# A list-scheduled two-layer encoder: input chunks loaded in natural order, and other priorities in the scheduler

## The chip, the core and the metric

One NeuronCore of a Trainium2 chip runs the whole program. PE (TensorE), DVE (VectorE), ACT (ScalarE) and POOL (GpSimd) each take their instructions in a fixed order; SP (SyncE) issues all DMAs, also in a fixed order. Time is device time of one execution in microseconds (us).

## What is computed

Two sequences of 1024 and 512 tokens get 16 meta tokens each and pass two layers of a hybrid encoder of width 1024. Each layer, cut to its core:

```python
h = rmsnorm(x, pre_g)
aq, ak, av, ag, bq, bk, bv, bg = split(h @ w_in)
oa = window_gqa_attention(rope(aq), rope(ak), av, sink) * silu(ag)   # 8 heads, 2 KV heads, window 128
ob = diff_attention(rope(bq), rope(bk), bv, lam, subln_g) * silu(bg) # 4 heads, softmax - lam * softmax
o = concat(oa, ob) @ w_out
x = x + rmsnorm(o, post_g)
```

All of it is in fp32. The outputs are the tokens without the meta tokens.

## The kernel before

**Tiles.** The 1568 tokens are cut into four chunks of 392. Every fp32 operand of a matmul is split into a high part and the rest, the low part (`hi`, `lo`), and a product is three matmuls: high times high, and high times low both ways. Activations of a chunk stand with their features on partitions (`hT[ci]`, in buffers named `slot`), weights in `whl` (high and low beside each other), two more of the first unit's weights in `kk` and `vv`.

**Stages.** A layer has six units: four heads of differential attention (`attn_b`), then two groups of window attention (`attn_a`). Before a unit comes its input projection (`inproj`, results in `ps_d`, now and then `ps_o`), four to six blocks of weights; its results go through rope or a gate to DRAM and come back as keys `kk`, values `vv` and queries `qq`. Scores stand in `ps_s`, transposes in `ps_t`, attention's products in `ps_o`; `pp` holds probabilities, `at` their transposes, `og` a unit's outputs, which go to `MX` in DRAM. Projections of the next unit fill PE while a unit's softmax runs. Then `outproj` runs steps that a string names: `b` is the first half of the output projection, `s` and `S` the second half with the row's statistics (`norm`), `l` loads half of a mix, `f` fetches the residual, `p` is the post norm with the residual and the next layer's row scale, `n` turns the new rows by transposes into layer 1's `hT`. So `n0` makes chunk 0 of layer 1, and it needs rows of output chunks 0 and 1.

**Start.** Chunk 0 of x is loaded with features on partitions. Its statistics come late and are multiplied in behind the projection (`late`). Before the change chunks 1 to 3 are loaded the same way; `prestats` squares them on ACT or POOL, sums the eight feature blocks on DVE, and `rstd_bc` turns the sums by PE transposes, reduces, takes the root on POOL, and turns them back into `rb`, a tile that has every token's scale on all partitions. `prenorm` then multiplies by gain and `rb` (DVE), copies the high part (ACT) and subtracts it (DVE).

**Order.** Nothing runs in the order of the code. `Recorder` notes every operation with what it depends on, and a list scheduler with modelled costs decides the order on each engine when the program is built: each engine takes the ready operation with the smallest `prio`, which is its place in the code less two numbers:

```python
o.prio = o.seq - self.boost - self.base + self.rnd.random() * SPREAD
```

`boost` is set around single operations (`BOOST_W` weights, `BOOST_M` mix loads, `BOOST_P` the first reading of a projection's result, `BOOST_E` the rest of its evacuation, rope above all), `base` for whole steps (`BASE`, `BASE_A` by unit, `BASE_0` and `BASE_S` for the statistics at the start). An operation made with `any`, `any_copy` or `any_tt` may go to either of two engines. Buffers are pools with fixed numbers of tiles. The profile names all instructions by one line, since one helper issues them; the tiles' names tell them apart.

Of the kernel before, what the change touches and what calls it, by code (L numbers as in the profile page):

```python
# [14 lines left out]
F32R = mybir.dt.float32r  # L15
# [18 lines left out]
    [[(0, 392)], [(392, 392)], [(784, 256), (1056, 120)], [(1176, 392)]],  # L34
# [6 lines left out]
BOOST_W = 300  # L41
BOOST_M = 1000
BOOST_E = 300
BOOST_P = 300
# [4 lines left out]
BASE_0 = 60  # L49
# [3 lines left out]
QUICK = 1  # L53
# [4 lines left out]
COMB = ((1, 1, 1, 1), (1, 1, 1, 1))  # L58
PRE_ACT = (0, 0, 0, 0, 0, 0, 0, 0)
# [4 lines left out]
ONLY = 4  # L64
# [63 lines left out]
ANY = dict(PE=0, ACT=0, DVE=0, POOL=0, SP=0)  # L128
# [414 lines left out]
def hymba_kernel(ctx, tc, xT, xr, w_in, w_out, rope, masks, pre_g, post_g, sub_g, sink_b, sink_m, lam_in, yo):  # L543
# [179 lines left out]
    def prestats(xs, tmp, n, only=False):  # L723
        if only:
            for i in range(4):
                r = slice(2 * (i % 2), 2 * (i % 2) + 2)
                x, y = xs[i // 2][:, r, 0:n], tmp[i // 2][:, r, 0:n]
                nc.any((nc.scalar, "activation", (y, x, AF.Square), {}),
                       (nc.gpsimd, "tensor_tensor", (y, x, x), dict(op=ALU.mult)))
                if i:  # L730
                    nc.vector.tensor_tensor(
                        tmp[0][:, 0:2, 0:n], tmp[0][:, 0:2, 0:n], tmp[i // 2][:, r, 0:n], op=ALU.add)
            nc.vector.tensor_tensor(tmp[0][:, 0, 0:n], tmp[0][:, 0, 0:n], tmp[0][:, 1, 0:n], op=ALU.add)
        else:
# [7 lines left out]
    def scaled(out, x, g, rb, n, act):
        for j in range(x.shape[1]):
            if act:
                nc.scalar.activation(out[:, j, 0:n], x[:, j, 0:n], AF.Copy, scale=g[:, j:j + 1])
                nc.any_tt(out[:, j, 0:n], out[:, j, 0:n], rb[:, 0:n], ALU.mult)
            else:
                nc.vector.scalar_tensor_tensor(
                    out[:, j, 0:n], x[:, j, 0:n], g[:, j:j + 1], rb[:, 0:n], op0=ALU.mult, op1=ALU.mult)

    def prenorm(l, ci, xs, rb, n):
        his, los = [], []
        for i in range(2):
            hi, lo = pair(F32R)
            for j in range(4):
                r = slice(j, j + 1)
                h = at_p([128, 1, CN])
                scaled(h, xs[i][:, r], preg[:, l, 4 * i + j:4 * i + j + 1], rb, n, PRE_ACT[2 * ci + i])
                h = h[:, :, 0:n]
                nc.any_copy(hi[:, r, 0:n], h)  # L760
                if l == 0 and ci < QUICK:
                    nc.vector.tensor_tensor(lo[:, r, 0:n], h, f32(hi[:, r, 0:n]), op=ALU.subtract)
                else:
                    nc.any_tt(lo[:, r, 0:n], h, f32(hi[:, r, 0:n]), ALU.subtract)
# [327 lines left out]
    def attn_a(l, g):  # L1092
        S = SC[l]
        AK, AV, AQ = S["AK"][g], S["AV"][g], S["AQ"][g]
        for s in range(2):
# [53 lines left out]
            for c0 in range(0, len(heads), 3):  # L1149
# [26 lines left out]
                nc.extra = [nc.last]  # L1176
# [133 lines left out]
    def outproj(l):  # L1310
# [91 lines left out]
        def stat(parts, M):  # L1402
            r = sm_p([128, 4])
            for u, p in enumerate(parts):
                sq = ru_p([128, 512])
                nc.scalar.activation(sq[0:M], p, AF.Square, scale=1.0 / 32, accum_out=r[0:M, u:u + 1])
            nc.vector.scalar_tensor_tensor(
                r[0:M, 2:3], r[0:M, 0:1], EPS, r[0:M, 1:2], op0=ALU.add, op1=ALU.add)
            nc.gpsimd.tensor_tensor(r[0:M, 3:4], r[0:M, 2:3], mhalf[0:M, 0:1], op=ALU.pow)
            return r[0:M, 3:4]  # L1410

# [186 lines left out]
```

## Time and profile before

| | |
|---|---|
| median of 3 runs | 1935.77 us (1933.12 to 1939.91) |
| profiled execution | 1938.61 us |
| its span | 1936.8 us |
| busy | PE 95%, DVE 78%, ACT 52%, POOL 14% |
| mean granted clock of PE | 0.985 |

The span runs from the first to the last instruction; the execution's time is 1.8 us more. A wait of PE is idle time with the tile and engine that ended it. The granted clock is a share of PE's full speed.

### The profile page before, as it was taken

The numbers are of one execution on the slowest core, as the hardware profiler recorded it, in microseconds if no ns is written. First come the engines' busy times: TensorE is split into PE (matmuls) and PEld (weight loads), VectorE is DVE, ScalarE is ACT, GpSimd is POOL, SyncE is SP. The second block draws the span as 40 slices with busy tenths as digits, with TensorE's granted clock in tenths as the row PEclk, the third lists the DMA queues.
The fourth block names the chain that finished last, engine by engine and source line by source line (L and its number), as shares of the span: only waits on it lengthen the run. The fifth ranks groups of instructions, "written<-read, shape, count | busy, mean of one in ns | idle before, by whom it ended". The sixth has DMA issues, their size and how long they took to land.

```text
span 1936.8 us, 35552 instructions
## 1 busy us (share of the span) xinstructions
PE 1843.4 (95%) x12328; PEld 1771.3 (91%) x12328; DVE 1515.2 (78%) x3363; ACT 1008.1 (52%) x2417; POOL 279.3 (14%) x516
## 2 busy tenths in 40 slices
PE   6999999999999989999789999999999999999998
PEld 5989989999989889999789999999999999889998
DVE  8858788888787787587988397787967859869767
ACT  4335445454444475575765254454545438648632
POOL 3001111211121210000221021121111101101001
PEclk8999999999999999999989999999999999999999
DMA  7253363544543657556354535445353475684464
GB/s 252 56 161 105 110 170 102 148 119 109 153 117 108 154 144 198 118 133 178 120 196 116 152 100 160 120 118 161 98 167 114 124 180 125 159 229 99 109 205 150
DMA packets 299147, 273.02 MB, mean 141 GB/s; under 512 B 101560, under 2 KB 263480, under 8 KB 298840
## 3 DMA queue, kind: packets, MB, share of 16 engines
q1 hardware_dynamic: 298968, 270.75, 50.5%
q8 instruction: 98, 1.61, 0.4%
q14 instruction: 81, 0.66, 0.1%
HBM read 149.19 MB, written 96.01 MB: 127 GB/s over the span
## 4 chain that ended last, share of the span: by engine, by line
PE 70%; DVE 11%; DMA 8%; ACT 4%; issue 4%; SPq 2%; POOL 1%; DVEq 0%; POOLq 0%; ACTq 0%
PE ps_d L451 43%; PE ps_s L451 10%; PE ps_o L451 9%; PE ps_t L451 8%; DVE at L451 2%; DVE pp L451 2%; DVE slot L451 2%; ACT pp L451 2%; SPq L451 2%; DVE sm L451 1%; DMA vv<-BV 1%; DVE og L451 1%; DMA kk<-AK 1%; DVE ru L451 1%; POOL sm L451 1%
## 5 line engine op out<-in xcount | busy, mean ns | idle before, releaser
L451 PE MATMUL ps_d<-slot,whl 128*128 128x392 f32 (+2 forms) x4560 | 938.2, 347 | 15.0 <-ACT slot L451 6.7
L451 PEld LDWEIGHTS ps_d<-slot,whl 128*128 128x128 f32 x4560 | 785.7, 190 | 22.2 <-ACT slot L451 6.7
L451 PE MATMUL ps_s<-kk,qq 128*128 128x264 f32 (+9 forms) x1496 | 284.4, 319 | 21.7 <-ACT pp L451 5.7
L451 PE MATMUL ps_o<-at,vv 128*128 128x256 f32 (+6 forms) x1368 | 285.9, 307 | 8.4 <-DVE og L451 5.5
L451 ACT ACTIVATE at<-ps_t 128x256 fp32r<-128x256 f32 (+9 forms) x434 | 187.7, 439 | 202.7 <-PE ps_t L451 177.4
L451 ACT ACTIVATE pp<-ps_s,sm 116x1040 f32<-116x1040 f32 (+4 forms) x208 | 203.9, 980 | 169.9 <-DVE sm L451 161.5
L451 DVE TENSOR_TENSOR at<-ps_t,at 128x256 fp32r<-128x256 f32 (+6 forms) x472 | 224.5, 480 | 68.0 <-ACT at L451 53.5
L451 PEld LDWEIGHTS ps_s<-kk,qq 128*128 128x128 f32 (+4 forms) x1496 | 227.2, 185 | 46.9 <-ACT pp L451 9.0
L451 PE MATMUL ps_d<-whl,slot 128*128 128x256 f32 x1800 | 259.0, 288 | 8.6 <-DVE slot L451 6.0
L451 PEld LDWEIGHTS ps_d<-whl,slot 128*128 128x128 f32 x1800 | 235.1, 192 | 14.3 <-DVE slot L451 7.2
L451 DVE TENSOR_REDUCE sm<-ps_s 116x1 f32<-116x1040 f32 (+4 forms) x208 | 218.3, 1050 | 34.3 <-PE ps_s L451 33.3
L451 ACT ACTIVATE pp<-pp,sm 128x336 f32<-128x336 f32 (+6 forms) x347 | 206.6, 607 | 61.0 <-DVE sm L451 57.6
L451 PEld LDWEIGHTS ps_o<-at,vv 128*128 128x128 f32 (+1 forms) x1368 | 214.0, 190 | 16.8 <-ACT pp L451 5.4
L451 PE MATMUL ps_t<-ident,pp 128*128 128x128 f32 (+6 forms) x1248 | 203.5, 269 | 3.1 <-DVE at L451 1.6
L451 POOL TENSOR_TENSOR pad<-pp,pad 128x64 fp32r<-128x64 f32 (+3 forms) x145 | 53.2, 370 | 819.0 <-ACT pad L451 528.1
L451 PEld LDWEIGHTS ps_t<-ident,pp 128*128 128x128 f32 (+6 forms) x1248 | 147.8, 137 | 14.7 <-ACT pp L451 2.8
L451 DVE CUSTOM_DVE_ANT_0 pp<-ps_s,mk,nsinks 128x336 f32<-128x336 f32 (+2 forms) x192 | 97.1, 528 | 22.1 <-PE ps_s L451 20.3
L451 POOL TENSOR_TENSOR sm<-sm 128x2 f32<-128x2 f32 (+3 forms) x112 | 48.7, 437 | 408.2 <-DVE sm L451 404.6
L451 POOL TENSOR_TENSOR sm<-sm,mhalf 128x1 f32<-128x1 f32 (+7 forms) x98 | 80.8, 830 | 132.9 <-DVE sm L451 129.6
L451 ACT ACTIVATE og<-ps_o 64x128 f32<-64x128 f32 (+4 forms) x248 | 66.1, 287 | 44.8 <-PE ps_o L451 27.3
L451 ACT ACTIVATE ru<-ps_d 128x392 f32<-128x392 f32 (+5 forms) x100 | 48.7, 487 | 73.9 <-PE ps_d L451 64.2
L451 DVE TENSOR_TENSOR slot<-slot 128x512 f32<-128x512 f32 (+3 forms) x79 | 73.9, 945 | 8.4 <-ACT slot L451 8.0
(158 smaller groups left out, 2130.3 us busy)
## 6 DMA issues: line engine op xcount, KB each, us to landing
wraw<-in_w_in_dram SPq DMA_DIRECT2D x46, 512.0 KB
qq<-qq SPq DMA_DIRECT2D x144, 128.0 KB
BS<-st SPq DMA_DIRECT2D x80, 196.0 KB
qq<-AQ SPq DMA_DIRECT2D x96, 128.0 KB
gl<-GT SPq DMA_DIRECT2D x72, 128.0 KB
MX<-og SPq DMA_DIRECT2D x72, 128.0 KB
slot<-MX SPq DMA_DIRECT2D x11, 768.0 KB
kk<-BS SPq DMA_DIRECT2D x8, 1040.0 KB
```

The source lines that it names most:

```text
L451: fn(*[_real(a) for a in args], **{k: _real(a) for k, a in kw.items()})
```

## The change

It has three parts.

1. Chunks 1 to 3 of x come from `xr`, with tokens on partitions: four tiles of 96 rows (chunks 1 and 2, which become 384 tokens long for layer 0) or 98 rows (chunk 3). `stat` makes each row's scale (two Squares with a running sum on ACT, one small step on DVE, one on POOL), two copies scale the tile, and `turned` turns it with PE: 8 groups of 4 transposes for a chunk. The high part is a copy of the result with the gain, the low part one DVE instruction. `turned` is what step `n` did before, now shared.
2. Numbers of the scheduler: `BOOST_W`, `BOOST_M`, `BOOST_E`, `BOOST_P`, `BASE_0`, `BASE`, `BASE_A`, `COMB` (how many row tiles of a head are combined with an ACT step), a penalty of 200 for DVE where an operation may go to two engines, and the modelled cost of DMAs by their number of rows.
3. In `attn_a` the mask steps no longer depend on the last score matmul of their batch, only on their own.

In all, PE has 96 transposes of chunks more and 24 of statistics fewer; columns of all other matmuls are the same. Instructions on DVE go from 3365 to 3298, on ACT from 1939 to 2012, on POOL from 521 to 535, on SP from 1550 to 1555.

```diff
-    [[(0, 392)], [(392, 392)], [(784, 256), (1056, 120)], [(1176, 392)]],
+    [[(0, 392)], [(392, 384)], [(776, 264), (1056, 120)], [(1176, 392)]],
...
-BOOST_W = 300
-BOOST_M = 1000
-BOOST_E = 300
-BOOST_P = 300
+BOOST_W = 280
+BOOST_M = 1200
+BOOST_E = -700
+BOOST_P = 1300
...
-COMB = ((1, 1, 1, 1), (1, 1, 1, 1))
+COMB = ((1, 1, 1, 3), (1, 1, 1, 1))
-BASE = ({'f': 400, 'p': 100, 's': -100, 'S': 0, 'b': 800}, {'f': 0, 'S': 400})
+BASE = ({'f': 400, 'p': 100, 's': -100, 'S': 0, 'b': 800, 'n': 100}, {'f': 0, 'S': 400})
-BASE_A = ((-200, 1500, 1500, -200, 200, 400), (0, 0, 0, 0, 1500, 0))
+BASE_A = ((-200, 1500, 1500, -200, 200, 400), (-300, 0, 0, 0, 1500, 0))
...
-ANY = dict(PE=0, ACT=0, DVE=0, POOL=0, SP=0)
+ANY = {'PE': 0, 'ACT': 0, 'DVE': 200, 'POOL': 0, 'SP': 0}
...
+                    dma(x[a:b].rearrange("p u d -> p (u d)"), xr[t0:t0 + b - a])
...
+    def stat(parts, M):
+        r = sm_p([128, 4])
+        for u, p in enumerate(parts):
+            sq = ru_p([128, 512])
+            nc.scalar.activation(sq[0:M], p, AF.Square, scale=1.0 / 32, accum_out=r[0:M, u:u + 1])
+        nc.vector.scalar_tensor_tensor(
+            r[0:M, 2:3], r[0:M, 0:1], EPS, r[0:M, 1:2], op0=ALU.add, op1=ALU.add)
+        nc.gpsimd.tensor_tensor(r[0:M, 3:4], r[0:M, 2:3], mhalf[0:M, 0:1], op=ALU.pow)
+        return r[0:M, 3:4]
+
+    def turned(l, tiles, off, n):
...
+                        nc.tensor.transpose(
+                            pt[:, o:o + M], get(u)[:, 128 * k:128 * k + 128], ident[0:M, 0:M])
...
+                nc.any_copy(hi[:, k, 0:n], p, g)
                 nc.vector.scalar_tensor_tensor(
+                    lo[:, k, 0:n], p, g, f32(hi[:, k, 0:n]), op0=ALU.mult, op1=ALU.subtract)
...
-                nc.extra = [nc.last]
                 for bi, (u, i) in enumerate(batch):
...
+            for x in xin[ci]:
+                r = stat([x[0:n // 4, u] for u in range(2)], n // 4)
+                for u in range(2):
+                    nc.any_copy(x[0:n // 4, u], x[0:n // 4, u], r)
```

The order on ACT at the start, from the first weight's high part (the first `whl<-pp`) on; `slot<-slot,preg` are chunk 0's high parts, `slot<-slot` squares of chunks 0 and 1. Before:

```order
L451 ACTIVATE whl<-pp 128x1024
L451 ACTIVATE slot<-slot,preg 128x392 x6
L451 ACTIVATE slot<-slot 128x784 x3
L451 ACTIVATE slot<-slot,preg 128x392 x2
L451 ACTIVATE slot<-slot 128x784 x2
L451 ACTIVATE whl<-pp 128x1024
L451 ACTIVATE kk<-pp 128x1024
L451 ACTIVATE vv<-pp 128x1024
```

After; `ru,sm<-slot` are the new Squares with a sum, on tiles of chunk 1:

```order
L448 ACTIVATE whl<-pp 128x1024
L448 ACTIVATE slot<-slot,preg 128x392 x6
L448 ACTIVATE slot<-slot 128x784 x3
L448 ACTIVATE slot<-slot,preg 128x392 x2
L448 ACTIVATE ru,sm<-slot 96x512 x5
L448 ACTIVATE whl<-pp 128x1024
L448 ACTIVATE slot<-slot,sm 96x512 x3
L448 ACTIVATE ru,sm<-slot 96x512 x2
L448 ACTIVATE kk<-pp 128x1024
```

Between chunk 0's last high part and the second weight's stand five Squares, where two squares of two blocks stood.

The order on PE at the start; `ps_d<-slot,whl`, `ps_o<-slot,kk` and `ps_d<-slot,vv` are products of the projection, `ps_t<-ident,sm` the statistics' way back. Before, from the last products of chunk 0 on:

```order
L451 MATMUL ps_d<-slot,vv 128x392 x18
L451 MATMUL ps_t<-ident,ru 98x128 x4
L451 MATMUL ps_t<-ident,slot 98x128 x4
L451 MATMUL ps_t<-ident,sm 128x98 x4
L451 MATMUL ps_t<-ident,slot 94x128 x4
L451 MATMUL ps_o<-slot,whl 128x392 x3
```

After, from the first instruction on; `ps_t<-ident,slot 128x96` are the new transposes of chunk 1:

```order
L448 MATMUL ps_d<-slot,whl 128x392 x24
L448 MATMUL ps_t<-ident,slot 98x128 x4
L448 MATMUL ps_d<-slot,whl 128x392 x9
L448 MATMUL ps_t<-ident,sm 128x98 x4
L448 MATMUL ps_d<-slot,whl 128x392 x9
L448 MATMUL ps_o<-slot,kk 128x392 x3
L448 MATMUL ps_d<-slot,whl 128x392 x3
L448 MATMUL ps_o<-slot,kk 128x392 x3
L448 MATMUL ps_t<-ident,slot 128x96 x8
```

Chunk 1's first instructions with its features stood behind all 96 products of chunk 0 with the four weights (the 18 above and 78 ahead of them), and stand behind 54 of them now.

The order on PE at the layer boundary, from the last products of attention (`ps_o`) to layer 1's first transposes (`ps_t<-ident,slot`); `ps_d<-whl,slot` and `ps_d<-whl,at` are products of the output projection, 128x256 each. Before:

```order
L451 MATMUL ps_o<-at,kk 128x256
L451 MATMUL ps_d<-whl,slot 128x256 x3
L451 MATMUL ps_o<-at,vv 128x512
L451 MATMUL ps_d<-whl,slot 128x256 x12
L451 MATMUL ps_t<-ident,slot 128x128 x12
L451 MATMUL ps_d<-whl,slot 128x256 x30
L451 MATMUL ps_t<-ident,slot 128x128 x8
```

After:

```order
L448 MATMUL ps_o<-at,vv 128x512
L448 MATMUL ps_d<-whl,slot 128x256 x21
L448 MATMUL ps_d<-whl,at 80x256 x24
L448 MATMUL ps_d<-whl,slot 128x256 x90
L448 MATMUL ps_d<-kk,at 80x256 x3
L448 MATMUL ps_d<-whl,slot 128x256 x3
L448 MATMUL ps_d<-kk,at 80x256 x3
L448 MATMUL ps_d<-whl,slot 128x256 x3
L448 MATMUL ps_d<-kk,at 80x256 x6
L448 MATMUL ps_d<-vv,at 80x256 x6
L448 MATMUL ps_d<-kk,slot 128x256 x3
L448 MATMUL ps_t<-ident,slot 128x128 x8
```

The transposes stood 12 matmuls behind the last product of attention, and stand 162 behind it now. Chunk 3's second mix half is first read in the 30 products that stood behind the first 12 transposes; after the change it is first read 115 products behind attention's last one.

The order on SP at the same place; `MX0<-og` stores attention's last outputs, `slot<-MX0` loads chunk 3's mix from them, `X1<-slot` stores rows of layer 0's result. Before:

```order
L451 DMA MX0_152<-og_11952 128x2x128
L451 DMA X1_137<-slot_10734 128x512
L451 DMA X1_137<-slot_10708 128x512
L451 DMA slot_12020<-MX0_152 128x4x384
L451 DMA pp_12024<-PM_138 80x1024
```

After:

```order
L448 DMA wraw_11968<-in_w_in_dram 128x1024
L448 DMA MX0_152<-og_11901 128x2x128
L448 DMA slot_12005<-MX0_152 128x4x384
L448 DMA X1_137<-slot_10815 128x512
L448 DMA pp_12022<-PM_138 80x1024
```

The two stores of X1 that stood between the store and the load are gone from there.

## Rows read from the trace of the kernel before

**Rows 1.** The page: busy time by engine, and the chain that ended last.
```profile
PE 1843.4 (95%) x12328; PEld 1771.3 (91%) x12328; DVE 1515.2 (78%) x3363; ACT 1008.1 (52%) x2417; POOL 279.3 (14%) x516
...
PE 70%; DVE 11%; DMA 8%; ACT 4%; issue 4%; SPq 2%; POOL 1%; DVEq 0%; POOLq 0%; ACTq 0%
```

**Rows 2.** Busy time by stage (windows: stretch, length, engines, PEclk, DMA).
```profile
0.00:120.50 120.50, 98.02 (x519) 92.99 (x520) 89.93 (x162) 43.79 (x72) 22.62 (x22) 0.94 0.54 170
...
640.00:935.00 295.00, 278.56 (x2013) 265.98 (x2012) 228.91 (x693) 187.28 (x542) 25.82 (x57) 0.98 0.60 152
935.00:985.00 50.00, 31.71 (x209) 27.70 (x208) 45.23 (x91) 33.55 (x82) 15.22 (x17) 0.83 0.55 175
985.00:1040.00 55.00, 53.61 (x404) 52.51 (x403) 47.23 (x91) 33.68 (x76) 10.70 (x14) 1.00 0.42 136
```

**Rows 3.** Timeline of PE at the start: time, length, work, idle time before it.
```profile
17.72 2.06 PE L451 MATMUL ps_d<-slot,whl 128*128 128x392 f32 x10 [1.40 <-DVE whl L451]
...
33.34 0.64 PE L451 MATMUL ps_t<-ident,ru 128*98 128x128 f32 x4 [1.42 <-DVE ru L451]
...
40.28 0.91 PE L451 MATMUL ps_t<-ident,sm 98*128 98x98 f32 x4 [5.76 <-POOL sm L451]
```

**Rows 4.** Windows behind the two longest waits, with the granted clock.
```profile
40.00:50.00 10.00, 8.70 (x29) 7.54 (x30) 8.24 (x16) 5.34 (x10) 1.68 (x2) 0.53 0.29 78
...
970.00:985.00 15.00, 8.92 (x39) 7.78 (x40) 11.64 (x19) 8.95 (x15) 2.01 (x3) 0.51 0.88 274
985.00:990.00 5.00, 5.00 (x46) 5.00 (x45) 3.45 (x6) 1.78 (x4) 0.00 (x0) 1.00 0.17 65
```

**Rows 5.** Timeline of PE at the layer boundary.
```profile
960.82 0.40 PE L451 MATMUL ps_o<-at,vv 80*128 80x512 f32 x1
961.05 1.59 PE L451 MATMUL ps_d<-whl,slot 128*128 128x256 f32 x12
...
970.42 1.59 PE L451 MATMUL ps_t<-ident,slot 128*128 128x128 f32 x6 [7.57 <-ACT slot L451]
975.50 1.09 PE L451 MATMUL ps_t<-ident,slot 128*128 128x128 f32 x4 [3.49 <-DVE slot L451]
977.60 0.79 PE L451 MATMUL ps_d<-whl,slot 128*128 128x256 f32 x2 [1.01 <-ACT slot L451]
979.55 5.82 PE L451 MATMUL ps_d<-whl,slot 128*128 128x256 f32 x28 [1.16 <-DVE slot L451]
```

**Rows 6.** Groups of instructions by form, PE, transposes of 98-row results.
```profile
L451 PE MATMUL ps_t<-ident,ru 128*98 128x128 f32 x140 | 21.2, 274 | 3.5 <-ACT ru L451 2.1 <-DVE ru L451 1.4
```

**Rows 7.** Groups by form, ACT: squares at the start, Squares with sum at the boundary.
```profile
L451 ACT ACTIVATE slot<-slot 128x784 f32<-128x784 f32 x8 | 6.4, 844 | 0.1
...
L451 ACT ACTIVATE ru<-slot 128x512 f32<-128x512 f32 x25 | 15.7, 627 | 6.5 <-DVE slot L451 6.2
...
L451 ACT ACTIVATION_READ_ACCUMULATOR ru<-slot 128x1 f32 x25 | 4.6, 186 | 0.0
```

**Rows 8.** Timeline of ACT and of DVE: chunk 3's second mix half.
```profile
976.06 1.48 ACT L451 ACTIVATE slot<-slot 128x1536 fp32r<-128x1536 f32 x1 [1.28 <-DMA slot<-MX]
...
977.75 1.75 DVE L451 TENSOR_TENSOR slot<-slot 128x1536 fp32r<-128x1536 f32 x1
```

**Rows 9.** Waits of PE, 640 to 935 us: total, times, longest.
```profile
PE ps_s L451 <- DMA kk<-AK: 4.6, 3, 2.5
PE ps_o L451 <- DVE og L451: 4.1, 5, 2.7
PE ps_s L451 <- DVE sm L451: 1.9, 3, 0.9
...
PE ps_t L451 <- DVE at L451: 1.3, 2, 1.0
PE ps_s L451 <- DMA qq<-qq: 1.0, 2, 0.6
```

**Rows 10.** Window 1010 to 1035 us, of instructions on transposes' results alone.
```profile
1010.00:1035.00 25.00, 6.72 (x48) 5.72 (x48) 9.13 (x16) 3.93 (x7) 1.00 0.40 125
```

More of the change, by code (lines that the diff above doesn't have):

```diff
@@ L597, in dma @@
             in_ = in_.bitcast(F32)
+        for v in (out, in_):
+            rows = [x for x in v.shape if x > 1] or [1]
+            nc.weight = max(nc.weight, cost * 16 // max(k for k in range(1, 17) if rows[0] % k == 0))
         nc.sync.dma_start(out=out, in_=in_)
@@ L742, in scaled, with prestats @@
[L742 to L747, printed above, removed]
-                nc.vector.scalar_tensor_tensor(
[L749 to L764, printed above, removed]
+    def prestats(xs, tmp, n):
+        for i in range(4):
+            r = slice(2 * (i % 2), 2 * (i % 2) + 2)
+            x, y = xs[i // 2][:, r, 0:n], tmp[i // 2][:, r, 0:n]
+            nc.any((nc.scalar, "activation", (y, x, AF.Square), {}),
+                   (nc.gpsimd, "tensor_tensor", (y, x, x), dict(op=ALU.mult)))
+            if i:
+                nc.vector.tensor_tensor(
+                    tmp[0][:, 0:2, 0:n], tmp[0][:, 0:2, 0:n], tmp[i // 2][:, r, 0:n], op=ALU.add)
+        nc.vector.tensor_tensor(tmp[0][:, 0, 0:n], tmp[0][:, 0, 0:n], tmp[0][:, 1, 0:n], op=ALU.add)
+        return rstd_bc(tmp[0][:, 0, 0:n], n, 1.0 / D)
@@ new lines, in stat @@
+    def stat(parts, M):
[8 more added lines that the diff above has]
+    def turned(l, tiles, off, n):
+        his, los = [], []
+        for u in range(2):
+            hi, lo = pair(F32R)
+            for k in range(4):
+                pt = ps_t([128, 512])
+                o = 0
+                with nc.macro():
+                    for get, M in tiles:
+                        nc.tensor.transpose(
+                            pt[:, o:o + M], get(u)[:, 128 * k:128 * k + 128], ident[0:M, 0:M])
+                        o += M
+                g = preg[:, l, 4 * u + k:4 * u + k + 1]
+                p = pt[:, off:off + n]
+                nc.any_copy(hi[:, k, 0:n], p, g)
+                nc.vector.scalar_tensor_tensor(
+                    lo[:, k, 0:n], p, g, f32(hi[:, k, 0:n]), op0=ALU.mult, op1=ALU.subtract)
@@ L765, in prenorm @@
             his.append(hi)
             los.append(lo)
-        hT[ci] = (rows(his, 4), rows(los, 4))
+        return rows(his, 4), rows(los, 4)
+    def prenorm(ci):
+        n = sum(m for _, m in ICH[0][ci])
+        m = n // 4
+        hT[ci] = turned(0, [(lambda u, x=x: x[0:m, u], m) for x in xin[ci]], 0, n)
     def load_w(src, pool=None, pri=0):
@@ L1400, in outproj @@
         rs = {}
[L1402 to L1410, printed above, removed]
         def norm(ci, j, M):
```

84 lines of the change are left out of this document (34 added, 50 removed).

## The prediction

> **What bounds the kernel now.** I read the page first, then the stages, then the single waits. PE is busy for 1843.4 us of the span of 1936.8 and holds 70% of the chain that ended last [rows 1]. So the time is PE's work plus PE's idle time, and the other engines matter only where PE waits for them. The stages show where that is [rows 2]: of 93 us of idle time, 22.5 lie in the first 120.5 us (120.5 − 98.02), 16.4 in layer 0's window attention (295 − 278.56), 18.3 in the 50 us in which layer 0's output projection turns into layer 1's input (50 − 31.71). The long stretches between have almost none, so a change of order can win nothing there.
>
> At the start the matmuls of chunk 0 with all four weights run on until 33.34 − 1.42 = 31.9 us; then PE waits 1.42 us for DVE and, a few transposes later, 5.76 us for POOL, which makes the reciprocal root of chunk 1's statistics [rows 3]. After that wait the granted clock is 0.53 between 40 and 50 us, near the lower level of 1.2 GHz [rows 4]. At the layer boundary four waits stand in a row: 7.57, 3.49, 1.01 and 1.16 us, 13.2 together [rows 5]. The first two are for the tiles that layer 1's first transposes read, the last two for the two parts of chunk 3's second mix half. Here too the clock falls, to 0.51 from 970 to 985, and is 1.00 behind it [rows 4].
>
> **The change, part by part.** *Input in natural order: what PE gains in work.* Chunks 1 to 3 are now turned by PE: 3 chunks x 8 column blocks x 4 tiles = 96 transposes more. The transposes of the column statistics, 4 out and 4 back per chunk, go: 24 fewer. The order shows both counts. The nearest row has 21.2 us for 140 transposes, 0.151 us each [rows 6], so +14.5 − 3.6 = +10.9. At 0.13 to 0.18 each it would be +9 to +13. Nothing hides this, since PE is the bound: it must be paid by waits.
>
> *What it takes off PE's waits.* The squares summed across eight blocks, the two transposes and the POOL step between give way to two Squares with a running sum per tile on ACT (0.627 + 0.186 us each [rows 7]), a POOL step and two scaled copies. Eight such Squares are 6.5 us of ACT for a chunk; before, four squares of 0.844 us [rows 7] did it on ACT and POOL, with three sums on DVE. But they need no transposes, so PE no longer waits in the middle of a chain for POOL. The first transposes of chunk 1 stand behind 54 projection matmuls, not 96: the rest of chunk 0's work serves as cover between chunk 1's pieces. The 5.76 and the 1.42 us should go, −7.2, and with them the low clock: 8.70 us of busy PE at 0.53 [rows 4] are 4.1 us of lost work, −4.1.
>
> *What it puts in front of the second weight.* PE waits 1.40 us at 17.72 for the low part of weight 1 [rows 3]. On ACT its high part now stands behind five of the new Squares, where two old ones stood (the excerpt shows it): 5 x 0.813 − 2 x 0.844 = +2.4 us [rows 7]. Behind it are queued weight 2 and the copies of chunk 1. DVE, which makes the low part, has one more sum of two blocks ahead of it, but is no longer slowed by POOL squaring chunk 1. Bounds +1 and +3; I take +2. Chunk 1's last tile could come up to 2 us late; the other chunks' projections can be put in between, so I take 0. The start: +10.9 − 7.2 − 4.1 + 2 = **+1.6**; −3 where the shorter waits go too, +12 where the low clock and a wait of the old size come back.
>
> *Layer boundary.* The stage priorities ('n' 100 ahead, mix loads at 1200, ropes and evacuations at −700) move the work. Before, 12 matmuls stand between the last attention product and layer 1's first transposes, and chunk 3's products come behind these. After, 162 output-projection matmuls stand there, and the first use of chunk 3's mix lies 115 behind that last product. The last attention product ends at 961.2. A matmul of this shape takes 1.59/12 = 0.133 us [rows 5]: 115 of them give 15.2 us and 162 give 21.5. When are the operands there? On the trace of before the last scaled tile is in use at 975.5, 14.3 us after that product, and the low part of chunk 3's mix is made by 977.75 + 1.75 = 979.5, 18.3 us after it [rows 5, 8]. So the transposes are covered (21.5 against 14.3) and chunk 3's mix nearly: 18.3 − 15.2 = 3.1 us of wait left. On SP the load of that mix now stands straight behind the store that it reads, where two X1 stores stood between; that is worth under 1 us and I leave it in the bounds. Of 13.2 us of waits 3.1 stay; the low clock goes with the long gap: 8.92 us at 0.51 [rows 4] are 4.4 lost. Together −10.1 − 4.4 = **−14.5**. Bounds: −17.6 with no wait left, −3 if the posts of chunk 0, now later in DVE's row, come last.
>
> *The rest of the tables, and the mask step.* Rope's second half, two or more DVE instructions per chunk and weight, now yields to attention's evacuations. PE waited 4.1 us for the `og` step and 1.3 us for `at` in layer 0's window attention [rows 9]; about half of that, −3, is what a better order on DVE can give. Free operations leave DVE for ACT by the 200 in the scheduler's table; ACT is under two thirds busy in that stage (187 of 295 us [rows 2]) and takes them. The mask step per head lets DVE begin before the last score matmul of a batch; PE's waits on `sm`, 1.9 us [rows 9], bound its gain, and I count nothing: DVE's own two steps behind it hold `ps_s` as long. `COMB` and `BASE_A` move work between engines that do not bind there. Bounds −8 and +5; I take **−3**.
>
> **Sum.** +1.6 − 14.5 − 3 = −15.9. The profiled execution took 1938.6, so 1922.7. It lay 2.8 above the median of the runs, 1935.8, so against runs the same sum gives 1919.9: I say **1920**.
>
> **A rule that speaks against it.** In this trace 48 transposes stand among projection matmuls from 1010 to 1035, 6.72 us of PE's work, and the granted clock is 1.00 throughout [rows 10]. The Trainium skill, "TensorE: Matmul & The Clock Gate", Part 4, says that a transpose does not count as PE activity in the way a matmul does and does not bring the clock up. By that rule the 96 transposes at the start, which stand in groups of 4 and 8 between 3 to 18 matmuls, might hold the clock low there; the row above speaks against it for such a mixture.
>
> **Rivals.**
> *A, the forecast:* 1913 to 1927.
> *B, more is won:* chunk 3's mix comes in time, the short waits before it (5.1 us of the 18.3 at the boundary) go too, and DVE's new order empties `og` and `at` in both layers. −17.6 − 5 − 8 + 1.6 − 2 (the first qq and ACT waits at the end of the start) = −31: about 1905. For it speaks that all of these are waits for DVE or ACT with PE work at hand; against it that DVE is 88% busy in the boundary's two stages (92.5 of 105 us [rows 2]).
> *C, DVE becomes the bound at the boundary:* in its two stages DVE works 45.23 + 47.23 = 92.5 us of 105 [rows 2]. Even without an idle moment the 105 could shrink only by 12.5, unless work leaves the stage; if DVE keeps half of its idle time, the gain is 6, the rest comes back as waits of chunks 1 to 3 of layer 1, and the sum is +1.6 − 6 − 1 = −5.4: 1930, and up to 1936 if the start costs more. The change moves some DVE work to ACT and some rope work out of it, so I hold A above it.
> *D, slower: rope comes too late.* With 1000 less in priority the ropes' ends, their stores and the loads of the next unit's keys and queries behind them on SP come later. PE already waits 4.6 us for `kk` and 1.0 for `qq` in one stage [rows 9], 2.5 at the longest. There are eleven unit starts behind the first; if each waits another 2.5 us it is +27 − 15.9: 1947. It decides from 1.5 us per start, where the whole gain is gone. Against it: the order leaves about the same number of matmuls between a unit's last projection and its first score as before.
> *E, the clock stays low at the start with the transposes:* chunk 1 to 3's transposes lie within some 50 us. If a third to a half of them ran at 0.53, 8 to 12 us would be lost that the forecast doesn't count: 1928 to 1932. The page's rule just named would bring it about; the row says that it does not in such a mixture.
> That the change does nothing is excluded: 72 more PE instructions and a new order on all engines.
>
> **How the numbers follow.** A 0.50, B 0.23, C 0.13, D 0.10, E 0.04. A measurement here can tell 0.3%, 5.8 us. A and B are faster; C and E mostly the same, D slower: faster 0.74, same 0.14, slower 0.12. The range leaves out half of B at its lower end and D at its upper end: 1904 to 1937. A's own range is 1913 to 1927.
>
> **What would show it.** Start: no wait of PE over 3 us behind the first 18 us, a clock of 1.00 in 35 to 55 us, PE's busy time about 7 us higher in the same stage. Boundary: no wait over 4 us behind the last attention product, no slice at the lower clock. Window attention: the `og` and `at` waits halved. I am wrong if PE waits long for weight 1 or for chunk 1's tiles (a start over 126 us), if waits for n1 to n3 appear behind 985 us, or if `kk` and `qq` waits grow at unit starts.

## The result, and the profile after

The changed kernel takes 1954.6 us (median, 1950.7 to 1958.5) against 1937.0 before: a ratio of 1.0092, interval 1.0064 to 1.012. It is slower by some 18 us, where a gain of 16 was forecast. The profiled execution spans 1951.7 us, 14.9 more than that of before. Its page:

```profile
PE 1855.2 (95%) x12400; PEld 1775.0 (91%) x12400; DVE 1486.4 (76%) x3296; ACT 1043.6 (53%) x2514; POOL 287.8 (15%) x530
```

PE is busy 11.8 us longer [rows 1], and its idle time, 93.4 before, is 96.5. So the work that the change adds was not paid by waits. (A stretch's idle time is its length less PE's busy time.) Five windows say where; they are cut at the first score of layer 0's heads, of its window attention, of layer 1's heads and of its window attention. The kernel before (stretch, length, engines, PEclk):

```profile
0.00:118.69 118.69, 97.48 (x517) 92.69 (x517) 88.95 (x161) 43.21 (x72) 22.62 (x22) 0.94 0.54 170
118.69:649.60 530.91, 518.14 (x3376) 498.37 (x3375) 426.10 (x807) 257.87 (x546) 92.12 (x182) 1.00 0.45 124
649.60:1097.33 447.73, 412.98 (x2908) 395.04 (x2909) 344.12 (x910) 268.69 (x717) 54.91 (x92) 0.97 0.56 153
1097.33:1589.07 491.74, 488.18 (x3177) 473.93 (x3177) 385.89 (x757) 239.02 (x511) 73.42 (x161) 1.00 0.48 133
1589.07:1936.80 347.73, 326.61 (x2354) 311.28 (x2353) 270.14 (x730) 199.33 (x572) 36.19 (x59) 0.98 0.55 153
```

The kernel after:

```profile
0.00:120.74 120.74, 101.74 (x589) 96.04 (x589) 71.34 (x150) 58.07 (x116) 14.60 (x24) 0.99 0.58 169
120.74:636.48 515.74, 510.58 (x3342) 493.66 (x3343) 415.53 (x789) 267.16 (x565) 91.90 (x183) 1.00 0.45 125
636.48:1088.03 451.55, 420.96 (x2950) 401.59 (x2949) 343.48 (x890) 269.79 (x738) 62.77 (x96) 0.98 0.57 153
1088.03:1598.44 510.41, 497.95 (x3215) 480.04 (x3216) 384.06 (x741) 248.76 (x527) 81.96 (x166) 1.00 0.47 130
1598.44:1951.70 353.26, 324.00 (x2310) 303.64 (x2308) 272.01 (x727) 199.83 (x568) 36.61 (x61) 0.98 0.53 149
```

Up to layer 1's first score the changed kernel is 9.3 us ahead (1088.03 against 1097.33), with 72 transposes more. Behind it, it loses 24.2: 863.7 us against 839.5 for practically the same number of matmuls (5525 against 5531). Idle time in layer 1 grows from 24.7 to 41.7; the other 7 us are longer busy time, which nothing here explains. The forecast's sum spoke of the first half. The loss is in the second, of which it said next to nothing: its reading that the long stretches have almost no idle time holds for the heads of layer 1 (3.6 us before), not for layer 1's window attention and output (21.1). It also had no term for layer 0's heads, which take 515.7 us in place of 530.9, with 34 matmuls fewer and idle time of 5.2 in place of 12.8.

The two places of the forecast, in windows that answer to [rows 2] and [rows 4], with one of all the new transposes (25 to 75 us) and one behind the boundary's longest wait (955 to 960):

```profile
25.00:75.00 50.00, 45.13 (x292) 41.73 (x292) 38.05 (x95) 29.53 (x64) 7.76 (x11) 1.00 0.39 99
40.00:50.00 10.00, 8.53 (x53) 7.97 (x52) 8.00 (x23) 7.38 (x17) 3.06 (x3) 1.00 0.37 84
935.00:985.00 50.00, 42.77 (x337) 41.20 (x336) 43.02 (x84) 35.55 (x82) 12.54 (x14) 0.97 0.60 192
955.00:960.00 5.00, 5.00 (x31) 4.96 (x30) 5.00 (x8) 2.27 (x6) 0.96 (x2) 0.66 0.40 133
960.00:975.00 15.00, 12.06 (x100) 11.65 (x99) 13.67 (x22) 12.52 (x27) 2.89 (x3) 1.00 1.00 328
```

The clock is 1.00 in the stretches that answer to those at 0.53 and 0.51, but it falls for a short time behind the boundary's longest wait, to 0.66 from 955 to 960. The boundary stage has 7.2 us of idle time where it had 18.3. Of the start's waits, in PE's timeline, those of 1.42 and 5.76 us [rows 3] are gone; between 20 us and the first score 2.32 us, for a chunk's low part, is the longest:

```profile
17.95 0.62 PE L448 MATMUL ps_d<-slot,whl 128*128 128x392 f32 x2 [1.06 <-ACT whl L448]
...
58.85 0.62 PE L448 MATMUL ps_d<-slot,whl 128*128 128x384 f32 x2 [2.32 <-DVE slot L448]
```

What is new stands in the list of PE's waits over the whole program (total, times, longest):

```profile
PE ps_s L448 <- DVE sm L448: 17.1, 26, 2.9
...
PE ps_s L448 <- DMA qq<-qq: 4.5, 4, 2.0
...
PE ps_s L448 <- DMA kk<-BS: 3.5, 4, 2.4
...
PE ps_o L448 <- DVE og L448: 2.5, 6, 0.6
PE ps_t L448 <- DVE at L448: 2.4, 4, 1.6
PE ps_s L448 <- DMA kk<-AK: 2.2, 3, 1.7
```

Scores wait 17.1 us for `sm`, the result of the mask steps, in 26 places, some 5.5 us of it in layer 0 and 11.7 in layer 1; before it was 1.9 in 3 [rows 9]. The waits for `og` are 2.5 in place of 5.5 over the whole program, those for `kk` and `qq` together 10.2 in place of 9.1.

### The profile page after: what moved, and what is told of

It is laid out like the page before. It is cut to its first block, busy times and chain, and to the rows that moved or that the text cites. A ratio compares the mean times of both kernels' runs of the same rounds, so it can differ in the third digit from the quotient of the medians.

```text
span 1951.7 us, 35826 instructions
## 1 busy us (share of the span) xinstructions
PE 1855.2 (95%) x12400; PEld 1775.0 (91%) x12400; DVE 1486.4 (76%) x3296; ACT 1043.6 (53%) x2514; POOL 287.8 (15%) x530
## 5 line engine op out<-in xcount | busy, mean ns | idle before, releaser
L448 PE MATMUL ps_s<-kk,qq 128*128 128x264 f32 (+9 forms) x1496 | 290.4, 321 | 33.0 <-DVE sm L448 17.1
L448 ACT ACTIVATE pp<-pp,sm 128x336 f32<-128x336 f32 (+7 forms) x372 | 223.5, 617 | 99.9 <-DVE sm L448 97.3
L448 PE MATMUL ps_d<-whl,slot 128*128 128x256 f32 x1800 | 263.0, 290 | 8.9 <-DVE slot L448 5.0
L448 PEld LDWEIGHTS ps_o<-at,vv 128*128 128x128 f32 (+1 forms) x1368 | 213.0, 189 | 15.2 <-DVE at L448 5.7
L448 PE MATMUL ps_t<-ident,pp 128*128 128x128 f32 (+6 forms) x1280 | 208.5, 270 | 5.2 <-DVE at L448 2.4
L448 POOL TENSOR_TENSOR pad<-pp,pad 128x64 fp32r<-128x64 f32 (+3 forms) x148 | 57.3, 392 | 830.0 <-ACT pad L448 503.6
L448 POOL TENSOR_TENSOR sm<-sm,mhalf 128x1 f32<-128x1 f32 (+8 forms) x107 | 88.5, 832 | 183.2 <-DVE sm L448 179.9
L448 POOL TENSOR_TENSOR sm<-sm 128x2 f32<-128x2 f32 (+2 forms) x112 | 50.9, 455 | 358.5 <-DVE sm L448 340.0
L448 ACT ACTIVATE og<-ps_o 64x128 f32<-64x128 f32 (+4 forms) x248 | 65.7, 286 | 44.4 <-PE ps_o L448 24.7
L448 ACT ACTIVATE ru<-slot 128x512 f32<-128x512 f32 (+1 forms) x82 | 51.1, 624 | 56.1 <-DVE slot L448 51.5
```

Source lines behind the costliest of these rows:

```text
L448: fn(*[_real(a) for a in args], **{k: _real(a) for k, a in kw.items()})
```

## The experiments

The change has three parts: I, the input in natural order; T, the scheduler's numbers; M, the mask step per head. Each experiment gives its ratio to the kernel before with the interval; two tables at the end have lengths and waits of all, and the pairs of kernels that one edit separates.

**M taken back (e1).**

```diff
+                nc.extra = [nc.last]
                 for bi, (u, i) in enumerate(batch):
```

> The changed kernel with the mask steps tied again to the last score matmul of their batch; nothing else undone. Theory M (mask per head costs: in the changed kernel PE waits 17.1 us for the masks' sums, before 1.9): 1938 to 1944 us against 1954.6, and the waits for the sums fall under 4 us. Theory R (the priorities cost: ropes come late, waits at units' starts and in layer 1's head stage, 12.5 us idle against 3.6): within 4 us of 1954.6, only the place of the waits moves. Theory I (the input's 96 transposes cost, PE is busy 11.8 us longer): within 4 us of 1954.6.

Measured 1965.6 us, 1.0141 (1.0122 to 1.0161): slower still by 11 us. The waits for the sums fell to 2.4 us, as theory M said, yet the time rose: the boundary's waits were back, 12.8 us in front of the transposes, and with them the low clock, 0.50 from 975 to 995 us. No theory had that.

**T taken back (e2).**

```diff
-BOOST_E = -700
-BOOST_P = 1300
+BOOST_E = 300
+BOOST_P = 300
...
```

All numbers of T, the penalty and the DMA costs go back with these two.

> The changed kernel with all numbers of the scheduler as before; natural order input and the mask step per head stay. Theory R: 1936 to 1945 us, layer 1's head stage is back at some 4 us of idle time. Theory M: 1950 to 1956, the 17 us of waits for the masks' sums stay. Theory I: 1950 and more, because the boundary's waits (13 us before) come back as well.

1957.3 us, 1.0104 (1.0084 to 1.0125), nearest to M. The sums' waits stay at 15.9 us. R falls as the sole cause. The boundary's waits, which I had come back under theory I, did not.

**I taken back (e3).**

```diff
-            prenorm(ci)
+            prenorm(0, ci, xin[ci], rb0[ci], sum(m for _, m in ICH[0][ci]))
```

The loads, squares and sums of before come with it.

> The changed kernel with the input of before (features on partitions, sums, two transposes); its numbers of the scheduler and the mask step per head stay. Theory I: 1940 to 1946 us, PE's busy time 10.9 us less. Theories M and R: 1950 to 1958; what the 72 transposes cost is paid back by the start's waits.

1974.0 us, 1.0191 (1.0165 to 1.0218), above every range: the natural order input is worth about 19 us to the changed kernel. Theory I falls.

**M alone (e4).**

```diff
-                nc.extra = [nc.last]
                 for bi, (u, i) in enumerate(batch):
```

> The kernel before with the mask step per head as its only change. Theory M: 1948 to 1954 us (before 1937), PE's waits for the masks' sums at 12 us or more. Theories R and I: 1933 to 1941.

1957.8 us, 1.0103 (1.0084 to 1.0122): 20 us for one line, 4 above M's range. Its scores wait for the masks 17.8 us in 26 places.

**I alone and T alone (e5, e6).** The other two parts, each by itself on the kernel before.

> The kernel before with the input in natural order as its only change (numbers of the scheduler and mask step as before). Theory M (masks per head cost about 20 us by themselves, since a later score of the same batch now waits for DVE) with T (the numbers cost in layer 1): 1925 to 1940 us, no wait for a mask inside a batch. Theory S (the order of before is a narrow optimum and nearly any other order of the same work costs 10 us or more): 1948 to 1965. Before: 1937.

1943.2 us, 1.002 (1.0002 to 1.0037): 3 us above the range of M with T, and 5 under S's.

> The kernel before with the new numbers of the scheduler as its only change. T: 1945 to 1960, of it 10 us or more in layer 1, at least half as idle time of PE. M alone: 1933 to 1941. S: 1948 to 1965, with the loss spread over both layers.

1977.9 us, 1.0192 (1.0165 to 1.0219): 39 us, more than T or S had. In layer 1 it loses 18.5 of them (858.0 against 839.5 for 5525 and 5531 matmuls), some 14 as idle time, as T had it; but the rest is lost up to layer 1's first score, so that the loss is spread over both layers, as S had it.

**A random order of neighbours (e7, e8).**

```diff
-SPREAD = 0
+SPREAD = 3
```

> The kernel before with a random 0 to 3 added to every operation's place in the scheduler's order (neighbours change places; engines, buffers and numbers as before). S: 1948 or more. M and T: 1932 to 1944.

1956.2 us, 1.0088 (1.0063 to 1.0112): 17 us for no change but the order of neighbours, in one such order.

> The changed kernel with the same random 0 to 3 added. S: anywhere from 1945 to 1970, up or down by several us from 1954.6, which shows how much of a difference an order by itself makes. M and T: within 4 us of 1954.6.

1949.6 us (1.0062, 1.0041 to 1.0083): 5 us less than the changed kernel. So an order by itself can be worth nearly as much here as the mask step alone (20), though not half of what all numbers cost alone (39). That sets a bound on what one run with one number undone can tell.

**Single numbers on the kernel before (g1 to g4).** g1:

```diff
-BOOST_E = 300
-BOOST_P = 300
+BOOST_E = -700
+BOOST_P = 1300
```

> The kernel before with BOOST_E at -700 and BOOST_P at 1300 as its only change. Theory R (rope later costs; the new numbers alone cost 39 us): 1960 to 1980 us against 1938, with PE waiting for ru and rw. Theory X (the penalty for DVE costs): 1932 to 1944. Theory S (any other order of the long stages costs 10 to 20 us, as the random order did with 17): 1948 to 1958.

1986.5 us, 1.0249 (1.0209 to 1.0289): 48 us, more than R had. Waits of PE, first two of the kernel before, then those of g1:

```profile
PE ps_o L451 <- DVE og L451: 5.5, 9, 2.7
...
PE ps_s L451 <- DMA qq<-qq: 4.0, 5, 1.3
```

```profile
PE ps_s L451 <- DMA qq<-qq: 8.7, 9, 2.9
PE ps_o L451 <- DVE og L451: 8.7, 12, 2.3
...
PE ps_d L451 <- DVE t L451: 8.0, 2, 4.5
...
PE ps_t L451 <- DVE st L451: 7.4, 5, 5.3
PE ps_d L451 <- DVE ru L451: 6.5, 8, 2.5
```

Before, the waits of `ps_d` for ru on DVE were 1.0 in all, and those for t and st on DVE 0.5 and 0.3. Late ropes make PE wait at results, buffers and queries: R by itself is shown.

g2, the penalty: `ANY = {..., 'DVE': 200, ...}`.

> The kernel before with the penalty of 200 for DVE on free operations as its only change; DVE's busy time falls by some 10 us. X: 1955 to 1975. R: 1932 to 1944. S: 1948 to 1958.

1955.7 us, 1.0086 (1.0057 to 1.0115): 17 us, in the ranges of X and of S, and the size of a random order, so it decides nothing. DVE's work goes down by 23 us and nothing is won with it.

g3, the boundary's own numbers:

```diff
-BOOST_M = 1000
+BOOST_M = 1200
-BASE = ({'f': 400, 'p': 100, 's': -100, 'S': 0, 'b': 800}, {'f': 0, 'S': 400})
+BASE = ({'f': 400, 'p': 100, 's': -100, 'S': 0, 'b': 800, 'n': 100}, {'f': 0, 'S': 400})
```

> The kernel before with 'n' at 100 and mix loads at 1200 as its only change: the order moves at the two output projections alone. The forecast's step on the boundary (other work between the last attention product and layer 1's transposes takes 10 us of waits and 4 of low clock away): 1923 to 1930. S, or a loss that comes back at the next chunks: 1934 to 1950.

1942.1 us, 1.0008 (0.999 to 1.0027): nothing. The waits of layer 1's first transposes stand as in [rows 5]:

```profile
971.85 0.47 PE L451 MATMUL ps_t<-ident,slot 128*128 128x128 f32 x1 [6.03 <-ACT slot L451]
974.56 1.33 PE L451 MATMUL ps_t<-ident,slot 128*128 128x128 f32 x5 [2.23 <-ACT slot L451]
979.53 1.08 PE L451 MATMUL ps_t<-ident,slot 128*128 128x128 f32 x4 [3.65 <-DVE slot L451]
```

g4: `BASE_A = (..., (-300, 0, 0, 0, 1500, 0))`.

> The kernel before with -300 for layer 1's first head as its only change: the order moves behind the boundary alone. If this number makes the loss in layer 1's head stage (9 to 12 us in every run with the new numbers): 1946 to 1952, all of it behind 1097 us. If not: 1935 to 1941. S: 1945 to 1958.

1953.0 us, 1.0069 (1.0046 to 1.0091): 15 us. The length up to layer 1's first score is that of before (1098.0); behind it 853.7 against 839.5.

**What holds inside the changed kernel (h1 to h4).** h1: `BOOST_E = BOOST_P = 300` in the changed kernel. h2: the same, and M taken back.

> The changed kernel with BOOST_E and BOOST_P at 300 again. R (late ropes cost in the changed kernel as they do alone, where they took 48 us): 1905 to 1935 us against 1954.6. S (the numbers don't add up; what an order costs hangs on the whole of it): 1942 to 1965.

1970.7 us, 1.0166 (1.0145 to 1.0188): slower than the changed kernel by 16, and above both ranges. R falls for the changed kernel: with masks per head the ropes' late place helps.

> The changed kernel with BOOST_E and BOOST_P at 300 and the mask steps tied to their batch again. R with M (the two parts that cost most alone, 48 and 20 us): 1915 to 1940. S: 1942 to 1965, as for the penalty for DVE (17) and layer 1's first head (15) alone.

1943.6 us, 1.0015 (0.9997 to 1.0034). From h1 to h2 one line wins 27 us. The sums' waits go from 20.9 to 1.2 us, the length of layer 1 from 863.4 to 843.2. The time is 4 us above the range of R with M and at the lower end of S's. What it shows is that I and the rest of T cost nothing that can be measured against the kernel before; on top of them ropes and masks each cost alone (22 us in e1, 27 in h1), and together 11.

h3 and h4 give each layer its own numbers and mask step ('n' and the modelled cost of DMAs stay new in both); h3's edit:

```diff
+NUMBERS = ((280, 1200, -700, 1300, {'DVE': 200}), (300, 1000, 300, 300, {}))
+MASK = (True, False)
...
+                nc.extra = [] if MASK[l] else [nc.last]
```

> The changed kernel in layer 0; in layer 1 the four boosts, the penalty for DVE, the mask step and BASE_A are as before. Theory L (by stages the changed kernel gains 9 us up to layer 1's first score and loses 24 behind it, so the loss is layer 1's): 1924 to 1934, with layer 1's two stages back at 840 us. S: 1940 to 1956, layer 1 loses about as much with any order it was not chosen with.

1939.6 us, 1.0005 (0.9985 to 1.0025).

> The other way round: natural order input, in layer 0 the boosts, penalty, mask step, COMB and BASE_0 as before, in layer 1 all as in the changed kernel. L: 1955 to 1968, 15 us and more of it in layer 1 against the run with the input alone (1943). S: 1945 to 1965, without a place.

1960.2 us, 1.0116 (1.0099 to 1.0132). h4's time lies in the ranges of L and of S, h3's 6 us above L's and just under S's; the times decide nothing by themselves, the place does. Taken out of layer 1 alone, the new numbers and masks give 15 us back, and the length behind layer 1's first score is 833.5 us for 5480 matmuls, in place of 863.7 for 5525; put there alone they cost 17 us against e5, and the length is 863.3. Theory L holds as to the place; its gain came out 6 us short.

**M in the last window group of layer 0 alone (k1, k2).**

```diff
+                nc.extra = [] if l == 0 and g == 1 else [nc.last]
```

> The changed kernel with BOOST_E and BOOST_P at 300, and the mask step per head in layer 0's second window group alone (elsewhere tied to its batch). Theory M2 (the mask step per head costs where scores of a batch wait for masks, 14 us in each layer's window attention, and wins 10 to 14 us at the layer boundary, since the last group's scores come earlier and more projection work is left behind them): 1925 to 1933 us against 1943.6 with no mask step per head; the boundary's waits of 17 us gone, waits for the masks' sums under 5 us. If the boundary's waits in the changed kernel were gone for another reason: 1940 to 1948. S: 1945 to 1960.

1931.3 us, 0.9962 (0.9948 to 0.9976): faster than both kernels. The transposes at the boundary in h2 and in k1, PE's timeline; h2 first:

```profile
955.19 0.48 PE L448 MATMUL ps_t<-ident,slot 128*128 128x128 f32 x1 [5.39 <-ACT slot L448]
961.38 1.33 PE L448 MATMUL ps_t<-ident,slot 128*128 128x128 f32 x5 [5.72 <-ACT slot L448]
964.91 1.09 PE L448 MATMUL ps_t<-ident,slot 128*128 128x128 f32 x4 [2.20 <-DVE slot L448]
```

k1:

```profile
968.76 0.49 PE L448 MATMUL ps_t<-ident,slot 128*128 128x128 f32 x3
970.73 0.77 PE L448 MATMUL ps_t<-ident,slot 128*128 128x128 f32 x5 [1.47 <-ACT slot L448]
...
975.55 1.04 PE L448 MATMUL ps_t<-ident,slot 128*128 128x128 f32 x8
```

A window around them, in h2 and then in k1:

```profile
950.00:990.00 40.00, 22.84 (x153) 21.48 (x154) 26.82 (x47) 19.73 (x44) 8.73 (x9) 0.70 0.48 157
```

```profile
950.00:990.00 40.00, 34.15 (x276) 32.78 (x276) 37.36 (x70) 29.53 (x67) 10.01 (x13) 0.99 0.63 210
```

In h2 they wait 13.3 us in three places, in k1 1.8 in all, and the granted clock around them is 0.99 in place of 0.70. M2 is borne out here, with two limits: of 17.4 us of waits between the last attention product and 1000 us in h2, 9.3 are left in k1, most of them at other places, and the scores' waits, 5.7 us, are a little more than it had. Its price of 14 us in each layer's window attention is not tested by k1. The gain of 12 us is one of medians. The two profiled executions last equally long (1931.1 and 1930.7), since h2's is the fastest of its ten.

> The kernel before with the natural order input and the mask step per head in layer 0's second window group alone. M2: 1926 to 1934 us against 1943 with the input alone. The other reason: 1940 to 1946. S: 1945 to 1960.

1941.0 us, 1.0013 (0.9996 to 1.003). The transposes' waits are gone too (12.2 us in e5, none here), but little time is won with them, 2 us against e5: the stage has other waits now (3.95 and 1.08 us for DVE near 1006 to 1019, 2.32 for a weight), and layer 1's heads wait 8.9 us in place of 5.5. On this point M2 named the wait rightly and the gain wrongly.

All of them, from the profiled execution of each (us; matmuls in parentheses; the cut is layer 1's first score). The profiled execution is faster than its kernel's median by 11 us in e5 and h2 and by 7 in h3, which makes their lengths short; in the others it lies within 3 us of it:

| kernel | parts | ratio | up to the cut | behind it | scores wait for `sm` | transposes wait at the boundary |
|---|---|---|---|---|---|---|
| before | none | 1 | 1097.3 (6801) | 839.5 (5531) | 1.9 | 11.1 |
| after | I T M | 1.0092 | 1088.0 (6881) | 863.7 (5525) | 17.1 | 0.5 |
| e1 | I T | 1.0141 | 1109.1 (6878) | 855.4 (5525) | 2.4 | 12.8 |
| e2 | I M | 1.0104 | 1104.4 (6924) | 850.6 (5481) | 15.9 | 0 |
| e3 | T M | 1.0191 | 1117.3 (6808) | 856.4 (5523) | 16.3 | 2.3 |
| e4 | M | 1.0103 | 1110.6 (6853) | 844.0 (5481) | 17.8 | 0 |
| e5 | I | 1.002 | 1092.1 (6876) | 838.3 (5532) | 2.3 | 12.2 |
| e6 | T | 1.0192 | 1120.7 (6806) | 858.0 (5525) | 3.3 | 12.8 |
| h1 | I T M, ropes old | 1.0166 | 1104.2 (6871) | 863.4 (5535) | 20.9 | 1.7 |
| h2 | I T, ropes old | 1.0015 | 1087.9 (6877) | 843.2 (5528) | 1.2 | 13.3 |
| h3 | I T M in layer 0 | 1.0005 | 1097.4 (6923) | 833.5 (5480) | 5.9 | 0.5 |
| h4 | I; T M in layer 1 | 1.0116 | 1093.0 (6877) | 863.3 (5528) | 10.9 | 12.5 |
| k1 | h2, M in one group | 0.9962 | 1082.1 (6878) | 848.6 (5529) | 5.7 | 1.8 |
| k2 | e5, M in one group | 1.0013 | 1102.0 (6924) | 837.9 (5481) | 6.1 | 0 |
| e7 | none, random order | 1.0088 | 1109.7 (6801) | 845.3 (5531) | 0.9 | 13.1 |
| e8 | I T M, random order | 1.0062 | 1091.8 (6879) | 853.2 (5524) | 13.9 | 0.7 |
| g1 | ropes' numbers | 1.0249 | 1133.2 (6800) | 853.6 (5535) | 2.0 | 14.5 |
| g2 | penalty | 1.0086 | 1108.9 (6802) | 842.6 (5531) | 0.2 | 13.3 |
| g3 | boundary's numbers | 1.0008 | 1101.1 (6801) | 840.4 (5531) | 1.1 | 11.9 |
| g4 | layer 1's first head | 1.0069 | 1098.0 (6801) | 853.7 (5531) | 1.8 | 11.1 |

Several of these kernels differ by one part alone. The same part, put into different kernels (differences of medians, us):

| part put in | from, to: difference |
|---|---|
| M | before, e4: +20; e5, e2: +14; h2, h1: +27; e6, e3: −4; e1, after: −11 |
| ropes' numbers | before, g1: +48; h2, e1: +22; h1, after: −16 |
| I | before, e5: +4; e4, e2: 0; e6, e1: −12; e3, after: −19 |

So no part has a price of its own. M costs 14 to 27 us with the ropes' old numbers; with the new ones it takes 11 off beside I, and 4 without I, which is within the spread of these runs.

## Why the prediction was wrong

**The step that failed is "The rest of the tables, and the mask step", −3, and in it the mask step, which was put at nothing:** "bound its gain, and I count nothing: DVE's own two steps behind it hold `ps_s` as long". It looked for a gain and set no price for a loss. Measured, the ropes' numbers and the mask step, all that the changed kernel has beyond h2, cost 11 us together. The mask step's price is in the order: with it, 33 scores in the changed kernel that are not the first of their batch have a wait on DVE's semaphore; in the kernel before, in e1 and in h2 there is none (36 in e4, 39 in h1, 14 in h3, 7 in k1). The three scores of a batch write three separate parts of one tile, `ps_s`. The scheduler compares the regions and sees no dependence between a mask on the first part and a score into the third. The built program waits. An example of layer 1 is the batch `ps_s_19838`; its scores and masks in the order of the changed kernel, with what each waits for, on PE and on DVE:

```
9036 L448 MATMUL ps_s_19838<-kk_19174,qq_19697 128x336 [waits DVE_49]
...
9042 L448 MATMUL ps_s_19838<-kk_19174,qq_19697 128x336 [waits DMAHW3_49]
9043 L448 MATMUL ps_s_19838<-kk_19174,qq_19697 128x336
9044 L448 MATMUL ps_s_19838<-kk_19174,qq_19697 128x336 [waits DVE_49]

2563 L448 ISA pp_19823,sm_19824<-ps_s_19838,mk_121,nsinks_132 128x336 [waits PE_49]
2565 L448 ISA pp_19856,sm_19824<-ps_s_19838,mk_121,nsinks_132 128x336 [waits PE_49]
```

The same batch in PE's timeline:

```profile
1612.54 0.47 PE L448 MATMUL ps_s<-kk,qq 128*128 128x336 f32 x2
...
1613.36 0.52 PE L448 MATMUL ps_s<-kk,qq 128*128 128x336 f32 x2
1616.78 0.58 PE L448 MATMUL ps_s<-kk,qq 128*128 128x336 f32 x2 [2.90 <-DVE sm L448]
```

And DVE's; its first line is the last mask of the batch before:

```profile
1611.77 0.57 DVE L448 CUSTOM_DVE_ANT_0 pp<-ps_s,mk,nsinks 128x336 f32<-128x336 f32 x1
...
1614.97 0.69 DVE L448 CAST whl<-wraw 128x1024 fp32r<-128x1024 f32 x1 [2.29 <-DMA wraw<-in_w_in_dram]
...
1616.15 0.57 DVE L448 CUSTOM_DVE_ANT_0 pp<-ps_s,mk,nsinks 128x336 f32<-128x336 f32 x1
1616.64 0.08 DVE L448 DVE_READ_ACCUMULATOR2_ANT sm<- 128x1 f32 x1
1617.39 0.57 DVE L448 CUSTOM_DVE_ANT_0 pp<-ps_s,mk,nsinks 128x336 f32<-128x336 f32 x1 [0.67 <-PE ps_s L448]
```

The third score (9044) starts at 1616.78, 0.06 us after the end of the accumulator's read at 1616.72, though that mask, the batch's first, reads another part of the tile. It stood on DVE behind a weight's copy, which itself waited 2.29 us for its load. And the next mask, at 1617.39, which reads the second part, waits 0.67 us for this score. So PE and DVE, which the masks behind the batch kept apart, now wait for each other in turn. In all 33 what the score waits for is the mask on an earlier part of its own tile; a tile for each head was not tried. The sum over PE's waits is +15.2 us. e4 has these waits without any other change, and is 20 us slower. In the changed kernel taking the line back wins nothing all the same (e1), since the boundary's gain goes with it.

**The boundary came out, for another reason.** Forecast −14.5: waits of 13.2 down to 3.1, and the clock up. Measured behind the last attention product: 7.7 us of waits, and 1.7 us lost at the low clock (5.00 us at 0.66) where 4.4 were, so about −8. Chunk 3's mix, for which the 3.1 stood, is read in the middle of the 42 products at 966.47 without a wait. What I didn't see is 4.02 us for a weight's low part, with the fall of the clock behind it, and two waits of 0.79 and 2.15 for DVE:

```profile
945.62 0.40 PE L448 MATMUL ps_o<-at,vv 80*128 80x512 f32 x1
945.85 2.66 PE L448 MATMUL ps_d<-whl,slot 128*128 128x256 f32 x21
...
954.50 2.04 PE L448 MATMUL ps_d<-whl,at 128*80 128x256 f32 x11 [4.02 <-DVE whl L448]
...
961.23 3.09 PE L448 MATMUL ps_d<-whl,slot 128*128 128x256 f32 x24 [0.79 <-DVE slot L448]
966.47 5.21 PE L448 MATMUL ps_d<-whl,slot 128*128 128x256 f32 x42 [2.15 <-DVE pp L448]
...
974.68 1.03 PE L448 MATMUL ps_t<-ident,slot 128*128 128x128 f32 x8
```

The transposes stand 28.7 us behind the last attention product (974.68 − 946.02), of which 7.2 are the waits above them; the 162 products take the 21.5 that were worked out, and the transposes wait 0.5 us in all. But the text gave this move to the numbers. 'n' and `BOOST_M` alone do nothing (g3), and with all numbers and no masks the transposes wait 12.8 us (e6). In all nine kernels with masks per head in layer 0's last window group the transposes wait 0 to 2.3 us in all; in all eleven without, 11.1 to 14.5. It is the mask step that brings attention's end forward in the order: in k1 159 products stand between that end and the transposes, in h2 none. So the part that I counted at nothing made both the gain at the boundary and the waits in the window stages.

**The start came out.** Forecast +1.6; the first score comes 2.05 us later. That the two lie so near is in part luck: the first score's place hangs on the order too, and it comes at 104.2 us with the input alone (e5, 510 matmuls up to it), at 136.9 with the numbers alone (e6, 600), at 120.7 with all (588). The transposes took less than I said:

```profile
L448 PE MATMUL ps_t<-ident,slot 96*128 96x96 f32 x64 | 7.7, 248 | 0.4 <-DVE slot L448 0.2
...
L448 PE MATMUL ps_t<-ident,pp 98*128 98x98 f32 x32 | 3.8, 247 | 0.0
```

11.5 us for 96, 0.12 each and not 0.15. (By the order the first of them stand behind 51 products of chunk 0, not 54.) Weight 1 was waited for 1.06 us for its high and 0.64 for its low part, 1.7 in all, not the 3.4 that the sum had. The low clock from 40 to 50 us is gone, but the clock is 0.83 from 20 to 30 us. Four waits of 0.6 to 2.3 us for later parts of the input are new, and the first score waits 2.37 us for the keys (before 1.27 for queries). As e5 and e3 show, the new input is near neutral alone (+4 us) and worth 19 us beside T and M. One gain of it had no term: PE's idle time in layer 0's heads is 5.2 to 8.2 us in the eleven kernels with the new input and 9.8 to 21.5 in the nine without.

**"The rest", −3, measured about +21** in the profiled executions (+14.9 − 2.05 + 8). Of it +15 are the waits for masks. The waits on `og` did halve, 5.5 to 2.5, while those for `at` on DVE rose from 2.2 to 4.2: the step had the one and not the other. Layer 0's heads won time, and layer 1's head stage lost it: 510.4 us for 3215 matmuls against 491.7 for 3177, with 8.9 us more of idle time in waits that are each under 1.6 us. h3 and h4 put it on the numbers in layer 1; g4 and g1 alone each give some 15 us in this stage, and with the ropes' numbers alone taken back (h1) it is 499.3 for 3177. Which wait begins it isn't settled: e7 has the same 15 us there with a random order, and h2, which keeps g4's number, has 495.1 for 3171. The order of before is narrow at this place, and theory S holds that far. It doesn't hold in general: e5, g3, h2, h3 and k2 have other orders and no loss over 0.3%, and k1 is faster.

**Rival D** was the right sign for a wrong reason. The ropes' numbers alone cost 48 us, more than the 27 that I gave it, but the waits for queries, 8.7 us in place of 4.0, are a small part of that. In the changed kernel the waits for keys and queries are 10.2 us against 9.1. The rule of the Trainium skill on transposes and the clock ("TensorE: Matmul & The Clock Gate", Part 4) did not come to bear: the granted clock is 1.00 from 25 to 75 us, where the 96 new transposes stand among the products.

## What to carry to other kernels

A dependence that is taken out of a scheduler's model is only gone if the built program drops it too: read the waits in the order before it is costed at nothing, and set a price for a loss as well as for a gain. Where a list scheduler decides, give a stage that the diff doesn't name a range of its own, since one random order of neighbours moved the time here by 17 us and by 5. Where parts act through one order, price them together: here the same line cost 27 us in one kernel and took 11 off another. And a part that loses overall may hold a gain at one place: kept in one group of layer 0 alone, the mask step gave the fastest kernel.

## What was not expected of the hardware

Executions of one program differ, and the granted clock differs with them, though not in step: ten of e5 took 1932.1 us (mean granted clock 0.989) to 1947.4 (0.984), with 1946.4 at 0.982. PE's order up to the first score is the same in the changed kernel and in e1; it took 120.7 us in the one and 123.9 in the other, which had a granted clock of 0.95 between 60 and 90 us where the first had 1.00. A small transpose costs less than a full one: in the changed kernel four in a row take 0.49 us on 96 rows and 0.60 on 128, both at a granted clock of 1.00.
